# 32x32 diagonal blocks solved on GpSimd and log decays by a masked scan in a gated DeltaNet + S5 layer, on one core

## The chip, the cores and the metric

One Trainium2 chip, of which the kernel uses one core. The metric is device microseconds of one execution, the median over several. Engines: TensorE (PE) multiplies matrices, VectorE (DVE), ScalarE (ACT) and GpSimd (POOL) do elementwise work, SyncE (SP) issues nearly all DMAs. Each engine runs its own queue strictly in the order in which the program was written; semaphores hold an instruction until what it needs is there.

## The reference

One hybrid layer on x of 1024 x 2048 floats: RMSNorm, one wide input projection, an S5 branch (diagonal state space, GELU, GLU) and a gated DeltaNet branch of 8 heads, both projected up, merged by gates, projected out, added to x and normalised. The part that the change touches is the chunked delta rule:

```python
gc = jnp.cumsum(g, axis=-1)
decay = jnp.exp(jnp.where(causal, gc[..., :, None] - gc[..., None, :], -jnp.inf))
kk = jnp.einsum("bhncd,bhnsd->bhncs", k, k)
a_mat = jnp.where(strict, beta[..., None] * kk * decay, 0.0)
rhs = jnp.concatenate([v * beta[..., None], k * (beta * jnp.exp(gc))[..., None]], axis=-1)
sol = lax.linalg.triangular_solve(a_mat, rhs, left_side=True, lower=True, unit_diagonal=True)
```

g is one log decay for each frame and head. `decay` is needed as a matrix for each chunk, and the unit lower triangular matrix 1 + a_mat has to be inverted or solved with. The kernel works in chunks of 128 frames (an exact regrouping of the reference's 64).

## The kernel before

The sequence goes in two passes of 512 frames (NPASS, T), that is four chunks of 128 frames. Within a pass the program walks over blocks of 128 output columns: first the small logits, then for each of the 8 heads the columns of k, q, v, z and two blocks of gates, with one block of the S5 input between; then further gates, the up-projections and the output projection. A block is 48 matmuls of 128x128 by 128x512 for K = 2048: weights are split in a high part (whi, cut by ScalarE) and a low part (wlo, the rest, by VectorE) in fp32r, so that each pair of tiles takes three matmuls. Weights come in halves of 512 KB (raw, three buffers, w_load). A half is two chunks; a chunk is one whi and one wlo of 128x512 and feeds 12 matmuls. w_prep makes chunks four ahead of their use, into five buffers.

All the rest is laid between these matmuls by generators in lanes ("prep", "chain", "s5" and others). pump() runs after every three matmuls and lets each lane take at most one step, up to its next yield. When a step may be taken is decided by Clock and Timed: a model that is kept while the program is written, with a time for each engine (fixed cost plus a cost an element from COST; for GpSimd 0.14 us and 2.1 ns an element for a tensor_tensor) and for each cell of each tile. After a step, its lane waits until the model's TensorE has passed the model's end of what the step issued, and 0.2 us more. The model's times thus set the order of the queues; the chip then runs that order with its own times.

The head's work is in two generators. d_prep(h) (lane "prep") makes ready what the recurrence needs; d_chain(h) (lane "chain") starts when it is done and walks the four chunks through the state. d_prep runs once for each head and pass, 16 times, in these stages:

- **Decay.** GpSimd makes dhl, the causal mask times the gate (once for the high and once for the low part, gth and gtl, two chunks at a time). TensorE multiplies it with after_r (four matmuls of 128x256), ScalarE takes the exponential into E, GpSimd masks E.
- **Products.** TensorE multiplies k with k and q; VectorE multiplies with E into LU and qk, and LU with cc_ (the product "M<-M,smalls" in the rows below).
- **Block solve.** LU (128 x 4 x 128) goes to DRAM (lu_d), and its 32 diagonal blocks of 16x16 come back, one in each of 32 partitions. GpSimd inverts all of them by forward substitution in 15 steps of two instructions. The inverses and their transposes go to DRAM (tu_d, two tensors) and come back as Tm and U, block diagonal.
- **Doubling.** From 16 to 32, 32 to 64 and 64 to 128: small matmuls with LU, Tm and U, and ScalarE copies of the results. The first of them (16 to 32) takes 16 matmuls of 32x32, two VectorE products (with off16 and id32), 32 more matmuls and eight ScalarE copies.

E, LU and mi are tiles of one head at a time; kq, v, qk, U and kd exist twice, for even and odd heads. All these are pieces of one block, which the profile's rows call M. A matmul in plain fp32 is two instructions in the profile. The helpers tt, ts and stt and the wrapper Timed record nearly every operation at one line, L135, so rows are told apart by tiles and shapes.

Of the kernel before, what the change touches and what calls it, by code (L numbers as in the profile page):

```python
# [36 lines left out]
P = 128  # L37
# [110 lines left out]
def kernel(  # L148
# [49 lines left out]
    def bank(i):  # L198
        return psum.tile([P, 512], F32, tag=f"p{i}", name=nm(f"p{i}"))
# [13 lines left out]
    def tt(o, a, b, op, eng=None):  # L213
        (eng or V).tensor_tensor(o, a, b, op=op)
# [24 lines left out]
    off16 = cpool.tile([P, 2, 16], F32, name="off16")  # L239
    id32 = cpool.tile([P, 32], F32, name="id32")  # L240
    G.memset(off16, 0.0)
    for b in range(4):
        s32 = slice(32 * b, 32 * b + 32)
        G.tensor_copy(id32[s32, :], ident[s32, s32])
        G.memset(off16[s32, 0, :], -1.0)
        G.affine_select(off16[s32, 0, :], off16[s32, 0, :], pattern=[[0, 16]], compare_op=ALU.is_ge,
                        fill=0.0, base=-16, channel_multiplier=1)
    after_r = cpool.tile([P, P], F32R, name="after_r")
    S.activation(after_r, after, AF.Copy)
# [27 lines left out]
    lu_d = [dram.tile([4, 129, P], F32, name=f"lu_d{i}") for i in range(2)]  # L277
    tu_d = [[dram.tile([4, 129, P], F32, name=f"tu_d{i}{j}") for j in range(2)] for i in range(2)]
# [738 lines left out]
    gth = cpool.tile([P, 8, 4], F32, name="gth")  # L1017
    gtl = cpool.tile([P, 8, 4], F32, name="gtl")
# [4 lines left out]
    def gates_prep(lg, ps_):  # L1023
# [50 lines left out]
    dhl = cpool.tile([P, 2, P], F32R, name="dhl")  # L1074
# [16 lines left out]
    def d_prep(h, ps_):  # L1091
# [54 lines left out]
        SP.dma_start(rows(lud), LU)  # L1146
        yield
        mif = mi.rearrange("p c n -> p (c n)")
        Ef = E.rearrange("p c n -> p (c n)")
        ba = mif[0:32, 0:256].rearrange("p (i m) -> p i m", i=16)  # L1150
        btm = mif[0:32, 256:512].rearrange("p (i m) -> p i m", i=16)
        bx = Ef[0:32, 0:256].rearrange("p (i m) -> p i m", i=16)
        bu = Ef[0:32, 256:512].rearrange("p (i m) -> p i m", i=16)
# [32 lines left out]
        g3 = mi[:, :, 0:32]  # L1186
        B4 = [slice(32 * b, 32 * b + 32) for b in range(4)]
# [504 lines left out]
```

## Time and profile before

| what | value |
|---|---|
| median of three runs | 2998.08 us (2997.61 to 3001.38) |
| the profiled execution | 3000.75 us, its span 2998.7 us |
| granted TensorE clock | 0.996 |
| DMA | 405.29 MB, 135 GB/s over the span |

The profiled execution's span is from its first to its last instruction; 2.05 us lie around it. Durations below come from that execution. In a row of the timeline stand the start (us), the time that the row covers, engine, line, operation, the tiles written and read, the shape, how many instructions the row merges, and in brackets how long the engine was idle before it and what ended that. In a row of a group stand, after the count, busy us and mean ns of one instruction, then idle time before such instructions and what ended it. TensorE's instructions are pipelined: what one costs is read from the distance of starts, not from its own duration.

### The profile page before, as it was taken

What the parts mean: (1) busy time and instruction counts of PE and PEld (TensorE: products, weight loads), DVE (VectorE), ACT (ScalarE), POOL (GpSimd) and SP (SyncE); (2) the same over time, 40 slices, a digit from 0 to 9 for tenths busy, and PEclk for the clock granted to TensorE, in tenths of its full rate; (3) what the DMA queues carried; (4) which work ended last, traced back from release to release, by engine and by line L of the source; (5) the groups of instructions that cost most, each with busy time, mean ns of one, the idle gap of its engine ahead of it and who ended that gap; (6) DMA issues with size and microseconds to landing.
All of it is one profiled execution on the core that took longest, in us unless ns stands there. A gap on an engine that the chain in (4) does not pass through costs nothing.

```text
span 2998.7 us, 42470 instructions
## 1 busy us (share of the span) xinstructions
PE 2952.0 (98%) x15902; PEld 2372.9 (79%) x15902; DVE 1676.4 (56%) x3130; ACT 1149.5 (38%) x2483; POOL 460.2 (15%) x857
## 2 busy tenths in 40 slices
PE   8999999999999999999999999999999999999998
PEld 6877777777777888888878777777777788888887
DVE  5746777777767422553454676567556633226542
ACT  5434544554544222334333344333433322223331
POOL 4413222122200000000024221222122000000000
PEclk9999999999999999999999999999999999999999
DMA  6435445444545644446354444544444464445541
GB/s 166 125 79 145 115 131 135 112 123 122 135 136 161 195 119 119 145 137 239 120 162 133 116 116 117 137 120 115 123 127 122 137 198 123 118 125 155 195 149 57
DMA packets 618240, 405.29 MB, mean 135 GB/s; under 512 B 91257, under 2 KB 551218, under 8 KB 616114
## 3 DMA queue, kind: packets, MB, share of 16 engines
q1 hardware_dynamic: 615730, 394.19, 46.2%
q0 software_dynamic: 2304, 8.39, 0.8%
q8 instruction: 125, 2.05, 0.3%
q14 instruction: 81, 0.66, 0.1%
HBM read 335.79 MB, written 66.72 MB: 134 GB/s over the span
## 4 chain that ended last, share of the span: by engine, by line
PE 85%; DVE 6%; ACT 3%; POOL 2%; DMA 2%; issue 2%; SPq 1%; DVEq 0%; POOLq 0%; ACTq 0%
PE p L135 85%; DVE G0a L135 2%; DVE M L135 2%; POOL M L135 2%; DVE wlo L135 1%; ACT M L135 1%; DVE tmp L135 1%; SPq L135 1%; POOL smalls L135 1%; DMA M<-tu_d 0%; ACT tmp L135 0%; ACT whi L135 0%; ACT L135 0%; ACT G0b L135 0%; DMA raw<-in_w_in_dram 0%
## 5 line engine op out<-in xcount | busy, mean ns | idle before, releaser
L135 PE MATMUL p<-X,whi 128*128 128x512 f32 (+1 forms) x4432 | 1396.4, 397 | 1.5 <-DVE whi L135 0.8
L135 DVE TENSOR_TENSOR wlo<-raw,whi 128x512 fp32r<-128x512 f32 x920 | 633.2, 700 | 744.2 <-ACT whi L135 743.5
L135 PEld LDWEIGHTS p<-X,whi 128*128 128x128 f32 (+1 forms) x4432 | 802.0, 188 | 175.3 <-issue 17.9
L135 PE MATMUL p<-X,wlo 128*128 128x512 f32 (+1 forms) x2184 | 852.7, 390 | 0.3 <-DVE wlo L135 0.2
L135 ACT ACTIVATE whi<-raw 128x512 fp32r<-128x512 f32 x917 | 557.8, 625 | 519.0 <-PE p L135 487.2
L135 PE MATMUL p<-Y,whi 128*128 128x512 f32 (+1 forms) x1808 | 568.0, 396 | 0.9 <-ACT p L135 0.9
L135 PEld LDWEIGHTS p<-X,wlo 128*128 128x128 f32 x2184 | 410.9, 188 | 89.1 <-DVE wlo L135 0.9
L135 PEld LDWEIGHTS p<-Y,whi 128*128 128x128 f32 (+1 forms) x1808 | 330.7, 187 | 71.3 <-issue 3.9
L135 PE MATMUL p<-Y,wlo 128*128 128x512 f32 x896 | 349.7, 390 | 0.0
L135 POOL TENSOR_SCALAR smalls<-smalls 128x4 f32<-128x4 f32 (+1 forms) x58 | 18.2, 313 | 1584.8 <-DVE smalls L135 1116.3
L135 ACT ACTIVATE tmp<-p 128x512 f32<-128x512 f32 x160 | 95.5, 597 | 400.9 <-PE p L135 393.6
L135 POOL TENSOR_TENSOR M<-M 32x28 f32<-32x28 f32 (+8 forms) x492 | 196.7, 400 | 282.8 <-DMA M<-lu_d 200.1
L135 DVE TENSOR_TENSOR G0a<-G0a 128x256 f32<-128x256 f32 (+1 forms) x432 | 211.1, 525 | 7.2 <-ACT G0a L135 3.5
L135 PEld LDWEIGHTS p<-M 32*32 32x32 f32 (+2 forms) x3072 | 153.0, 123 | 72.6 <-ACT M L135 28.8
L135 PEld LDWEIGHTS p<-Y,wlo 128*128 128x128 f32 x896 | 168.1, 188 | 36.5 <-DVE wlo L135 0.4
L135 PE MATMUL p<-M 32*32 32x32 f32 (+3 forms) x3072 | 186.9, 215 | 6.9 <-DMA M<-tu_d 3.8
L135 ACT ACTIVATE M<-p 32x128 f32<-32x128 f32 (+3 forms) x337 | 98.9, 297 | 161.1 <-PE p L135 157.5
L135 DVE SCALAR_TENSOR_TENSOR tmp<-tmp,vec 128x512 f32<-128x512 f32 x144 | 112.0, 778 | 11.7 <-ACT tmp L135 8.3
L135 DVE TENSOR_TENSOR G0a<-p,G0a 128x512 f32<-128x512 f32 x128 | 82.0, 681 | 13.9 <-PE p L135 13.8
L135 DVE TENSOR_TENSOR_SCAN G0a<-rho,scar,G0a 128x256 f32<-128x256 f32 x128 | 89.3, 738 | 0.0
L135 PE MATMUL p<-whi,G0a 128*128 128x512 f32 x280 | 88.5, 391 | 0.0
L135 PE MATMUL p<-whi,X 128*128 128x512 f32 x256 | 82.2, 393 | 0.0
(209 smaller groups left out, 2640.7 us busy)
## 6 DMA issues: line engine op xcount, KB each, us to landing
raw<-in_w_in_dram SPq DMA_DIRECT2D x324, 512.0 KB, 4.0
raw<-in_w_out_dram SPq DMA_DIRECT2D x56, 512.0 KB, 4.0
raw<-in_dn_w_up_dram SPq DMA_DIRECT2D x32, 512.0 KB, 4.1
raw<-in_s_w_up_dram SPq DMA_DIRECT2D x32, 512.0 KB, 3.9
td_d<-tmp SPq DMA_DIRECT2D x32, 256.0 KB, 2.0
M<-tu_d SPq DMA_DIRECT2D x32, 256.0 KB, 3.2
cs_d<-G0a SPq DMA_DIRECT2D x32, 256.0 KB, 2.2
yg_d<-G0a SPq DMA_DIRECT2D x64, 128.0 KB, 2.4
```

What stands on the lines that cost most here:

```text
L135: return f(*a, **k)
```

## The change

Four things change, all in or around d_prep.

- **Decay by a scan.** gates_prep transposes the gates of all heads and chunks (128x32) on TensorE and writes them as rows to a small DRAM tensor, g_d. For each head one DMA reads the head's 512 gates into E, replicated over 128 partitions. VectorE then runs a tensor_tensor_scan over each chunk: state = (state + g) * strict, with strict the mask of later frames. dhl, its products on GpSimd and the four matmuls with after_r go, as do gth and gtl.
- **Blocks of 32.** The diagonal blocks are 32x32, 16 of them. Four DMAs write them to lu_d. One DMA reads each whole block (4 KB) into 8 partitions, 128 partitions in all, into E and mi together (Emi). Each partition holds four columns of the inverse, which start as columns of the identity, read from idg_d. GpSimd runs the forward substitution in 31 steps of two instructions.
- **The way back.** One DMA writes the result to tu_d, now one tensor, and one reads it as U. VectorE transposes U in blocks of 32x32 into Tm.
- **The stage from 16 to 32 goes**, with off16 and id32.

COST, LATE and WAIT, from which the order follows, stay as they were.

```diff
@@ gates_prep
-        S.activation(gth.bitcast(F32R), gt, AF.Copy)
-        tt(gtl, gt, gth, SUB, eng=G)
         p3 = bank(5)
-        for i, m in enumerate((causal, after_r.bitcast(F32), ones)):
+        PE.transpose(p3[0:32, 96:96 + P], gf, ident)
+        for i, m in enumerate((causal, afterk, ones)):
             PE.matmul(p3[:, i * 32:(i + 1) * 32], lhsT=m, rhs=gf, start=True, stop=True)
+        grow = mif[0:32, 256:256 + P]
+        S.activation(grow, p3[0:32, 96:96 + P], AF.Copy)
+        SP.dma_start(g_d[0], grow)
@@ d_prep
-        pD = bank(5)
-        for j in range(2):
-            for i, gg in enumerate((gth, gtl)):
-                tt(dhl, gg[:, h, 2 * j:2 * j + 2].unsqueeze(2).broadcast_to([P, 2, P]),
-                   causal[:, None, :].broadcast_to([P, 2, P]), MUL, eng=G)
-                yield
-                PE.matmul(pD[:, j * 256:(j + 1) * 256], lhsT=after_r, rhs=dhl.rearrange("p c n -> p (c n)"),
-                          start=(i == 0), stop=(i == 1))
-        S.activation(E.rearrange("p c n -> p (c n)"), pD, AF.Exp)
+        Ef = E.rearrange("p c n -> p (c n)")
+        SP.dma_start(Ef, part(g_d, h * 512, (0, P), (1, 512)))
+        yield
+        for c in range(4):
+            V.tensor_tensor_scan(E[:, c, :], E[:, c, :], strict, 0.0, op0=ADD, op1=MUL)
+        S.activation(Ef, Ef, AF.Exp)
         tt(E, E, hb4(causal), MUL, eng=G)
...
-        SP.dma_start(rows(lud), LU)
-        yield
...
-        SP.dma_start(ba, diag_blocks(lud))
-        G.memset(mif[0:32, 256:512], 0.0)
-        G.memset(mif[0:32, 256:512:17], 1.0)
-        yield
-        for j in range(15):
-            n = 15 - j
-            a = ba[:, j, j + 1:16].unsqueeze(2).broadcast_to([32, n, j + 1])
-            b = btm[:, j:j + 1, 0:j + 1].broadcast_to([32, n, j + 1])
-            tt(bx[:, 0:n, 0:j + 1], a, b, MUL, eng=G)
-            tt(btm[:, j + 1:16, 0:j + 1], btm[:, j + 1:16, 0:j + 1], bx[:, 0:n, 0:j + 1], SUB, eng=G)
+        for b in range(4):
+            SP.dma_start(part(lud, b * 1024, (32, 32), (4096, 4), (1, 32)),
+                         LU[32 * b:32 * b + 32, :, 32 * b:32 * b + 32])
+        yield
+        lb = dw["Emi"].rearrange("p (j t) -> p j t", j=32)
+        Uf = U.rearrange("p c n -> p (c n)")
+        iu, ix = (Uf[:, i * P:(i + 1) * P].rearrange("p (m t) -> p m t", m=4) for i in range(2))
+        SP.dma_start(dw["Emi"], part(lud, 0, (1024, 16), (0, 8), (1, 1024)))
+        SP.dma_start(Uf[:, 0:P], part(idg_d, 0, (0, 16), (P, 8), (1, P)))
+        yield
+        for j in range(31):
+            n = 31 - j
+            a = lb[:, j:j + 1, j + 1:32].broadcast_to([P, 4, n])
+            b = iu[:, :, j:j + 1].broadcast_to([P, 4, n])
+            tt(ix[:, :, 0:n], a, b, MUL, eng=G)
+            tt(iu[:, :, j + 1:32], iu[:, :, j + 1:32], ix[:, :, 0:n], SUB, eng=G)
             if j % 3 == 2:
                 yield
-        G.tensor_copy(bu, btm.rearrange("p i m -> p m i"))
-        yield
-        SP.dma_start(diag_blocks(tud[0]), btm)
-        SP.dma_start(diag_blocks(tud[1]), bu)
+        SP.dma_start(part(tud, 0, (4128, 16), (512, 8), (P, 4), (1, 32)), iu)
         stored = clock.last
...
-        SP.dma_start(Tm, rows(tud[0]))
-        SP.dma_start(U, rows(tud[1]))
-        yield
-        pG = bank(5)
+        SP.dma_start(U, rows(tud))
+        yield
+        V.transpose(Tm.rearrange("p c n -> p (c n)"), U.rearrange("p c n -> p (c n)"))
         gs = mi
-        for b in B4:
-            for c in range(4):
-                PE.matmul(pG[b, c * 32:(c + 1) * 32], lhsT=LU[b, c, b], rhs=Tm[b, c, b], start=True, stop=True)
-        tt(g3, pG[:, 0:P].rearrange("p (c n) -> p c n", c=4),
-           off16.rearrange("p a c -> p (a c)")[:, None, :].broadcast_to([P, 4, 32]), MUL)
-        tt(g3, g3, id32[:, None, :].broadcast_to([P, 4, 32]), ADD)
-        yield
-        pU = bank(2)
-        for b in B4:
-            for c in range(4):
-                PE.matmul(pU[b, c * 32:(c + 1) * 32], lhsT=g3[b, c, :], rhs=U[b, c, b], start=True, stop=True)
-                PE.matmul(pU[b, P + c * 32:P + (c + 1) * 32], lhsT=U[b, c, b], rhs=g3[b, c, :],
-                          start=True, stop=True)
-        for b in B4:
-            S.activation(U[b, :, b], pU[b, 0:P].rearrange("p (c n) -> p c n", c=4), AF.Copy)
-        for b in B4:
-            S.activation(Tm[b, :, b], pU[b, P:2 * P].rearrange("p (c n) -> p c n", c=4), AF.Copy)
         yield
```

**Where it moves instructions.** Three places in the last head of the second pass. First VectorE's queue before, from the LU product (first row) to the products on the first doubling matmuls; "M" is d_prep's block, "smalls" holds the factors cc_, "off" and "id" are off16 and id32:

```order
L135 TENSOR_TENSOR M_1692_13095<-M_1692_13095,smalls 128x512
...
L135 TENSOR_TENSOR wlo_19523<-raw_19398,whi_19522 128x512
...
L135 TENSOR_TENSOR wlo_19746<-raw_19626,whi_19745 128x512
L135 TENSOR_TENSOR wlo_19764<-raw_19626,whi_19763 128x512
L135 TENSOR_TENSOR M_1692_13095<-p_2508_19770,off_86 128x4x32
L135 TENSOR_TENSOR M_1692_13095<-M_1692_13095,id_87 128x4x32
```

And the same stretch of VectorE's queue after the change, from the LU product to the transpose that makes Tm:

```order
L135 TENSOR_TENSOR M_1668_12823<-M_1668_12823,smalls 128x512
...
L135 TENSOR_TENSOR wlo_18999<-raw_18814,whi_18998 128x512
...
L135 TENSOR_TENSOR wlo_19342<-raw_19241,whi_19341 128x512
L135 TENSOR_TENSOR M_1668_12823<-p_2469_19348,smalls 128x512
L135 TENSOR_TENSOR wlo_19366<-raw_19241,whi_19365 128x512
L135 STREAM_TRANSPOSE M_1668_12823<-M_1668_12823 128x512
```

Between the two ends stand 10 wlo rows before and 15 now (first and last are shown; an S5 head's work stands among them in both). The products with off and id are gone.

Second, SyncE's queue in the same head before, from the write of LU to the reads of the inverses; "raw" are weight halves:

```order
L135 DMA lu_d_125<-M_1692_13095 128x4x128
L135 DMA G0a_12942<-cs_d 128x512
L135 DMA M_1692_13095<-lu_d_125 32x16x16
L135 DMA raw_19570<-in_w_in_dram 128x8x128
...
L135 DMA raw_19690<-in_w_in_dram 128x8x128
L135 DMA tu_d_128<-M_1692_13095 32x16x16
L135 DMA tu_d_129<-M_1692_13095 32x16x16
L135 DMA yg_d<-G0a_12942 64x2x256 x4
L135 DMA M_1692_13095<-tu_d_128 128x4x128
L135 DMA M_1692_13095<-tu_d_129 128x4x128
```

And after:

```order
L135 DMA lu_d_112<-M_1668_12823 32x4x32 x4
L135 DMA raw_19023<-in_w_in_dram 128x8x128
L135 DMA M_1668_12823<-lu_d_112 128x1x1024
L135 DMA M_1668_12823<-idg_d 128x1x128
...
L135 DMA raw_19071<-in_w_in_dram 128x8x128
...
L135 DMA raw_19290<-in_w_in_dram 128x8x128
L135 DMA tu_d_114<-M_1668_12823 16x32x32
L135 DMA raw_19339<-in_w_in_dram 128x8x128
L135 DMA M_1668_12823<-tu_d_114 128x4x128
```

Three weight halves stood between the read of LU and the reads of the inverses, six stand there now, one of them between the write and the read.

Third, TensorE's queue before, where the result of the solve is first used ("p" is PSUM, 32x32 rows are the small matmuls, the others belong to the projection):

```order
L135 MATMUL p_2508_19770<-M_1692_13095 32x32 x16
L135 MATMUL p_2505_19762<-Y_1453_11621,whi_19692 128x512 x2
...
L135 MATMUL p_2509_19799<-M_1692_13095 32x32 x32
L135 MATMUL p_2505_19762<-Y_1453_11621,whi_19715 128x512 x2
...
L135 MATMUL p_2513_19855<-M_1692_13095 32x32 x8
```

And after:

```order
L135 MATMUL p_2470_19364<-Y_1429_11349,wlo_19315 128x512
L135 MATMUL p_2476_19396<-M_1668_12823 32x32 x8
L135 MATMUL p_2470_19364<-Y_1429_11349,whi_19314 128x512 x2
...
L135 MATMUL p_2477_19413<-M_1668_12823 32x32 x16
```

The groups of 16 and 32 small matmuls are gone; the group of 8, from 32 to 64, is now the first that uses the result.

More of the change, by code (lines that the diff above doesn't have):

```diff
@@ L238 @@
                     channel_multiplier=1)
[L239 to L249, printed above, removed]
+    afterk = cpool.tile([P, P], F32, name="afterk")
+    S.activation(afterk, after, AF.Copy)
+    strict = cpool.tile([P, P], F32, name="strict")
+    tt(strict, causal, ident, SUB, eng=G)
     halfpi = cpool.tile([P, 1], F32, name="halfpi")
@@ L275 @@
     cs_d = dram.tile([32, P, 512], F32, name="cs_d")
-    lu_d = [dram.tile([4, 129, P], F32, name=f"lu_d{i}") for i in range(2)]
-    tu_d = [[dram.tile([4, 129, P], F32, name=f"tu_d{i}{j}") for j in range(2)] for i in range(2)]
+    lu_d = [dram.tile([4, 4, 1024], F32, name=f"lu_d{i}") for i in range(2)]
+    tu_d = [dram.tile([4, 129, P], F32, name=f"tu_d{i}") for i in range(2)]
+    idg_d = dram.tile([1, 32, 32], F32, name="idg_d")
+    g_d = dram.tile([1, 32, P], F32, name="g_d")
     nq_d = [dram.tile([1, P, 16], F32, name=f"nq_d{i}") for i in range(2)]
@@ L287, in part @@
         return bass.AP(tensor=a.tensor, offset=a.offset + off, ap=[list(x) for x in dims])
-    def diag_blocks(d):
-        a = d[:, :, :]
-        return bass.AP(tensor=a.tensor, offset=a.offset, ap=[[16 * P + 16, 32], [P, 16], [1, 16]])
     def rows(d):
@@ L1009, in d_views @@
             dw["set"].append(s)
-        dw["E"] = tk(512).rearrange("p (c n) -> p c n", c=4)
         dw["LU"] = tk(512).rearrange("p (c n) -> p c n", c=4)
-        dw["mi"] = tk(512).rearrange("p (c n) -> p c n", c=4)
+        dw["Emi"] = tk(1024)
+        dw["E"] = dw["Emi"][:, 0:512].rearrange("p (c n) -> p c n", c=4)
+        dw["mi"] = dw["Emi"][:, 512:1024].rearrange("p (c n) -> p c n", c=4)
         dw["ch"] = tk(512)
     gt = cpool.tile([P, 8, 4], F32, name="gt")
-    gth = cpool.tile([P, 8, 4], F32, name="gth")
-    gtl = cpool.tile([P, 8, 4], F32, name="gtl")
     bt = cpool.tile([P, 8, 4], F32, name="bt")
@@ L1072, in gates_prep @@
         yield -1
-    dhl = cpool.tile([P, 2, P], F32R, name="dhl")
     nk = [small(f"nk{i}", 4) for i in range(2)]
@@ L1145, in d_prep @@
         yield
-        SP.dma_start(rows(lud), LU)
+        for b in range(4):
+            SP.dma_start(part(lud, b * 1024, (32, 32), (4096, 4), (1, 32)),
+                         LU[32 * b:32 * b + 32, :, 32 * b:32 * b + 32])
         yield
[L1148 to L1153, printed above, removed]
-        SP.dma_start(ba, diag_blocks(lud))
-        G.memset(mif[0:32, 256:512], 0.0)
-        G.memset(mif[0:32, 256:512:17], 1.0)
-        yield
-        for j in range(15):
-            n = 15 - j
-            a = ba[:, j, j + 1:16].unsqueeze(2).broadcast_to([32, n, j + 1])
-            b = btm[:, j:j + 1, 0:j + 1].broadcast_to([32, n, j + 1])
-            tt(bx[:, 0:n, 0:j + 1], a, b, MUL, eng=G)
-            tt(btm[:, j + 1:16, 0:j + 1], btm[:, j + 1:16, 0:j + 1], bx[:, 0:n, 0:j + 1], SUB, eng=G)
+        lb = dw["Emi"].rearrange("p (j t) -> p j t", j=32)
[3 more added lines that the diff above has]
+        SP.dma_start(Uf[:, 0:P], part(idg_d, 0, (0, 16), (P, 8), (1, P)))
+        yield
+        for j in range(31):
[4 more added lines that the diff above has]
+            tt(iu[:, :, j + 1:32], iu[:, :, j + 1:32], ix[:, :, 0:n], SUB, eng=G)
             if j % 3 == 2:
                 yield
-        G.tensor_copy(bu, btm.rearrange("p i m -> p m i"))
-        yield
-        SP.dma_start(diag_blocks(tud[0]), btm)
-        SP.dma_start(diag_blocks(tud[1]), bu)
+        SP.dma_start(part(tud, 0, (4128, 16), (512, 8), (P, 4), (1, 32)), iu)
         stored = clock.last
@@ L1179, in d_prep @@
         yield stored
-        SP.dma_start(Tm, rows(tud[0]))
-        SP.dma_start(U, rows(tud[1]))
+        SP.dma_start(U, rows(tud))
         yield
-        pG = bank(5)
+        V.transpose(Tm.rearrange("p c n -> p (c n)"), U.rearrange("p c n -> p (c n)"))
         gs = mi
-        g3 = mi[:, :, 0:32]
-        B4 = [slice(32 * b, 32 * b + 32) for b in range(4)]
-        for b in B4:
-            for c in range(4):
-                PE.matmul(pG[b, c * 32:(c + 1) * 32], lhsT=LU[b, c, b], rhs=Tm[b, c, b], start=True, stop=True)
-        tt(g3, pG[:, 0:P].rearrange("p (c n) -> p c n", c=4),
-           off16.rearrange("p a c -> p (a c)")[:, None, :].broadcast_to([P, 4, 32]), MUL)
-        tt(g3, g3, id32[:, None, :].broadcast_to([P, 4, 32]), ADD)
-        yield
-        pU = bank(2)
-        for b in B4:
-            for c in range(4):
-                PE.matmul(pU[b, c * 32:(c + 1) * 32], lhsT=g3[b, c, :], rhs=U[b, c, b], start=True, stop=True)
-                PE.matmul(pU[b, P + c * 32:P + (c + 1) * 32], lhsT=U[b, c, b], rhs=g3[b, c, :],
-                          start=True, stop=True)
-        for b in B4:
-            S.activation(U[b, :, b], pU[b, 0:P].rearrange("p (c n) -> p c n", c=4), AF.Copy)
-        for b in B4:
-            S.activation(Tm[b, :, b], pU[b, P:2 * P].rearrange("p (c n) -> p c n", c=4), AF.Copy)
         yield
@@ L1323, in zero_tu @@
     def zero_tu():
-        for a in tu_d:
-            for b in a:
-                SP.dma_start(rows(b), ztile.rearrange("p (c n) -> p c n", c=4))
+        for b in tu_d:
+            SP.dma_start(rows(b), ztile.rearrange("p (c n) -> p c n", c=4))
+        SP.dma_start(idg_d[0], ident[0:32, 0:32])
     def out_gen(yr, oss, r0):
```

## The prediction

> **What bounds the kernel now.** I read the page first, then who waits for whom, then TensorE's own timeline.
>
> ```profile
> span 2998.7 us, 42470 instructions
> PE 2952.0 (98%) x15902; PEld 2372.9 (79%) x15902; DVE 1676.4 (56%) x3130; ACT 1149.5 (38%) x2483; POOL 460.2 (15%) x857
> PE   8999999999999999999999999999999999999998
> PE 85%; DVE 6%; ACT 3%; POOL 2%; DMA 2%; issue 2%; SPq 1%; DVEq 0%; POOLq 0%; ACTq 0%
> ```
>
> TensorE (PE) is busy in every slice and carries 85% of the chain that ended last. VectorE (DVE) and GpSimd (POOL) have room. So two things count: how long PE stands on work that goes, and where PE will newly wait.
>
> ```profile
> PE p L135 <- DMA M<-tu_d: 3.8, 5, 0.8
> PEld p L135 <- POOL dhl L135: 6.2, 15, 0.8
> PEld p L135 <- ACT whi L135: 8.5, 22, 0.9
> ```
>
> These are the only PE waits near the change: us in total, times, the longest. PE almost never waits for the solve's result (tu_d), so the order around it fits the machine, but by how much it fits has to be found.
>
> **What PE gets back.** PE's rows in one head of the first pass:
>
> ```profile
> 423.74 0.39 PE L135 MATMUL p<-X,wlo 128*128 128x512 f32 x1
> 424.06 0.89 PE L135 MATMUL p<-M 32*32 32x32 f32 x32
> 424.88 0.73 PE L135 MATMUL p<-X,whi 128*128 128x512 f32 x2
> ...
> 427.41 0.40 PE L135 MATMUL p<-X,wlo 128*128 128x512 f32 x1
> 427.74 1.91 PE L135 MATMUL p<-M 32*32 32x32 f32 x64
> 429.57 0.73 PE L135 MATMUL p<-X,whi 128*128 128x512 f32 x2
> ...
> 430.37 0.63 PE L135 MATMUL p<-X,whi 128*128 128x512 f32 x2
> 430.84 0.39 PE L135 MATMUL p<-X,wlo 128*128 128x512 f32 x1
> 431.06 0.62 PE L135 MATMUL p<-X,whi 128*128 128x512 f32 x2
> ```
>
> Three projection matmuls start 0.69 us apart (430.37 to 431.06), so one costs 0.23. The group of 32 instructions (16 matmuls, two instructions each) costs 424.88 - 423.74 - 0.23 = 0.91 us of PE's time, the group of 64 costs 429.57 - 427.41 - 0.23 = 1.93. Both go, in 16 heads: 16 x 2.84 = **45.4 us**.
>
> The decay matrix loses four 128x256 matmuls a head, 64 in all. Each is half as wide as a projection matmul, 0.11 us: 7.2, and with the 6.2 us of waits for dhl **13.4 us**. The 3.8 us of waits for tu_d go too, but the same transfer is waited for in another place, below. Sum: 62.6 us. The transpose of the gates that gates_prep gains is one small matmul a pass, nothing here.
>
> **What the new solve takes on POOL.** It replaces 30 instructions of 15 to 64 elements by 62 of 4 x n elements, n from 31 to 1 (2 x 4 x 496 = 3968 elements). No row shows a form of that kind; the nearest:
>
> ```profile
> 1593.37 0.61 POOL L135 TENSOR_TENSOR dhl<-gth,causal 128x256 fp32r<-128x256 f32 x1 [0.90 <-PE p L135]
> 1599.05 1.02 POOL L135 TENSOR_TENSOR smalls<-smalls,minus 128x4 f32<-128x4 f32 x1
> 1600.15 0.20 POOL L135 TENSOR_TENSOR smalls<-smalls,bt 128x4 f32<-128x4 f32 x1
> 1620.07 11.53 POOL L135 TENSOR_TENSOR M<-M 32x15 f32<-32x15 f32 x30 [17.57 <-DMA M<-lu_d]
> 1886.09 14.79 POOL L135 TENSOR_TENSOR M<-M 32x15 f32<-32x15 f32 x30 [15.91 <-DMA M<-lu_d]
> 2287.39 14.52 POOL L135 TENSOR_TENSOR M<-M 32x15 f32<-32x15 f32 x30 [17.76 <-DMA M<-lu_d]
> ```
>
> A product of 4 elements takes 0.20 us, one of 256 takes 0.61: 1.63 ns an element on 0.19, and 0.08 between two (1599.05 + 1.02 to 1600.15). By that the old 30 (1360 elements) take 30 x 0.27 + 2.2 = 10.3 us, the new 62 take 62 x 0.27 + 6.5 = 23.3. The old ones really take 11.5 to 14.8, and DVE's load says why:
>
> ```profile
> 312.00:344.00 32.00, 32.00 (x273) 24.98 (x272) 25.71 (x55) 16.78 (x35) 13.34 (x32) 1.00 0.45 129
> 1620.00:1631.60 11.60, 11.60 (x55) 9.18 (x54) 2.71 (x5) 2.73 (x5) 9.25 (x30) 1.00 0.91 275
> 1886.00:1901.00 15.00, 15.00 (x73) 11.83 (x72) 7.82 (x15) 5.60 (x10) 12.57 (x31) 1.00 0.49 141
> 2288.00:2318.00 30.00, 29.16 (x230) 23.12 (x229) 12.08 (x22) 10.32 (x24) 12.67 (x30) 1.00 0.57 157
> ```
>
> The columns are the stretch, its length, then busy time of PE, PEld, DVE, ACT and POOL. With DVE busy 2.71 us the 30 lose 1.2 us against 10.3, with 7.82 they lose 4.5: about 0.5 us for each us of DVE. The 30 us that the new solve would fill in a late head have 12.08 us of DVE, so 23.3 + 5.5 = **28.8 us** in the second pass. In the first pass DVE is twice as busy (25.71 in 32), but POOL already shares with it at the worst rate seen, 14.8 / 10.3 = 1.43; I take 1.36, **31.8 us**. Bounds: 23.3 if nothing collides, 33.4 if everything does at 1.43.
>
> The Trainium skill, "GPSIMD Engine Reference", section 3.1 (Elementwise — side-by-side cycle accounting), puts a two-input GpSimd operation at about 2.6 cycles an element, 2.2 ns at the page's 1.2 GHz. Against the 1.63 ns of these rows its estimate for the solve would be some 2 us longer; the rows decide.
>
> **How long the order lets it take.** VectorE makes one wlo for every 12 projection matmuls, 12 x 0.23 = 2.7 us of PE, so its queue is a clock. In the last head 10 wlo rows stand between the LU product (M<-M,smalls) and the first use of the solve's result (M<-p,off): 27 us. After the change 15 rows stand between the LU product and the new transpose. Counted over the heads: before 9 to 11 (one head 14), after 13, 24, 15, 15, 16, 17, 16, 16 in the first pass and 16, 15, 16, 15, 15, 15, 15, 15 in the second. 15 rows are 40.8 us, and the first matmul on the result stands 0.7 us further on: 41.5.
>
> ```profile
> 2281.14 0.40 SPq L135 DMA_DIRECT2D lu_d<-M  x1
> 2285.39 0.32 SPq L135 DMA_DIRECT2D M<-lu_d  x1
> 2306.00 1.14 SPq L135 DMA_DIRECT2D M<-tu_d  x2
> 2309.26 0.87 PE L135 MATMUL p<-M 32*32 32x32 f32 x32 [0.84 <-DMA M<-tu_d]
> raw<-in_w_in_dram SPq DMA_DIRECT2D x324, 512.0 KB, 4.0
> M<-tu_d SPq DMA_DIRECT2D x32, 256.0 KB, 3.2
> tu_d<-M SPq DMA_DIRECT2D x32, 32.0 KB, 1.7
> L135 DVE STREAM_TRANSPOSE M<-M 128x512 f32<-128x512 f32 x16 | 11.2, 701 | 0.0
> L135 DVE TENSOR_TENSOR_SCAN G0a<-rho,scar,G0a 128x256 f32<-128x256 f32 x128 | 89.3, 738 | 0.0
> ```
>
> Today: 2281.14 to 2309.26 is 28.1 us, and PE waits the last 0.84. The clock of rows is right within 1 us. After the change the same way is: four small LU writes, 0.4 apart, the last landing 1.7 later (2.9); the 512 KB replicated read (4.0 like a weight load); POOL; the write (1.7) and one 256 KB read (3.2); the transpose (0.7); some 0.9 between steps. That is 13.4 us beside POOL: 42.2 in the second pass, 45.2 in the first. Against 41.5 PE is 0.7 late in each of six second-pass heads, 4 us. In the first pass: the first head (13 rows, 36.1 us; before the S5 work fills DVE, so at 42.2) 6 late, two heads with 15 rows 3.7 each, three with 16 rows (44.2) 1.0 each, the two with 17 and 24 none: 16. As a row count is cut off by half a row (1.3 us) on average, part of that is not there. I take **12 us** of new waits, ends 0 (POOL 23.3) and 66 (POOL 33.4: 37 in the second pass, 29 in the first).
>
> The Clock itself gives the solve only 62 x 0.14 us + 3968 x 2.1 ns = 17 us. The order leaves more, because three of its steps are handed out at a time, between groups of PE work, and each batch waits for the Clock's PE to pass the one before. While PE waits for the solve, its own queue stands still. Behind the transposing DVE stand the wlo of chunks that PE needs four chunks (11 us) later, so a lateness under that costs PE once. Behind the solve's write SyncE has one weight load and the read of the result; that load is needed three halves later, 16 us, against 4 to land.
>
> **The rest, costed at nothing.** DVE gains four scans (half of 738 ns each) and a transpose, loses two small products: 1.6 us a head on an engine at 56%. ACT loses eight copies; PE waited 8.5 us for ACT in all, so the gain is between 0 and that. The decay load (256 KB, about 3.2 us) is issued as soon as the head before has freed E, and hidden by that lead; if it were not, the chain of the head before would stand behind the scans on DVE, at most 16 x 3.2 = 51 us. POOL loses the dhl products.
>
> **Sum.** The profiled run took 3000.75 us, 2.05 around its span. 3000.75 - 62.6 + 12 = 2950; that run is 2.67 over the median of the three, so **2947 us**.
>
> **Rivals.** *The solve is late everywhere and PE hands back the gain* (slower). For: POOL stretched by 1.43 beside a busy DVE, and longer operations meet more DVE instructions. Against: behind today's solve DVE is lightly loaded (12.08 in 30 us). The point is a solve of about 33 us, 0.53 us an instruction with its gap: then the waits reach 60 us, 2996. At 36 us it is 3 more in 15 heads, 3041. The Trainium skill, "SBUF — State Buffer" (SBUF: two separate sides), says that a DVE operation with two SBUF inputs and a GpSimd operation hold a shared port pair by turns, each for a whole instruction. The stretched runs agree; how far it reaches with the new form no run here shows.
>
> *Late in part*: solves of 30.5 to 33 us, or the decay load showing: 27 to 58 us of waits, 2962 to 2993.
>
> *No change*: what goes on PE is filled by another bound, such as weights through ACT and DVE. Against it stands a PE that waits 8.5 us for ACT in 2998. 2998.
>
> **Chances.** Forecast (2935 to 2960) 0.60, late in part 0.18, no change 0.08, slower 0.14. A measurement of this kernel tells some 0.2% (6 us) from no change. Faster 0.78, same 0.08, slower 0.14. The range runs from 2932 (no waits, and some of ACT's gain) to 2996.
>
> **What would show it.** The costliest-groups view of TensorE:
>
> ```profile
> L135 PE MATMUL p<-M 32*32 32x32 f32 x2304 | 64.1, 193 | 4.1 <-DMA M<-tu_d 3.8 <-ACT M L135 0.2
> ```
>
> This group falls from 2304 to 768 instructions (24 of 72 matmuls a head stay), with none on dhl. The solve's 62 instructions take 27 to 32 us a head. PE's (or DVE's) wait for M<-tu_d stays near a us a head. I am wrong if that wait is over 4 us a head, if single new POOL instructions pass 0.5 us, or if wlo waits grow.

## The result, and the profile after

| | median of its runs, us | against before, 95% interval |
|---|---|---|
| before | 2999.02 (2997.61 to 3001.38) | |
| changed | 3018.4 (3013.54 to 3023.04) | 1.0064 (1.0041 to 1.0086) |

The changed kernel is 19 us slower; 2947 was forecast, and the range ended at 2996. The profiled execution took 3022.74 us. Its page: span, busy time of each engine, and the shares of the chain that ended last.

```profile
span 3019.6 us, 39590 instructions
PE 2941.1 (97%) x14304; PEld 2361.7 (78%) x14304; DVE 1706.5 (57%) x3178; ACT 1104.5 (37%) x2349; POOL 625.1 (21%) x1243
PE 62%; POOL 14%; DVE 9%; DMA 7%; issue 5%; ACT 2%; SPq 1%; DVEq 0%; POOLq 0%; ACTq 0%
```

1598 TensorE instructions are gone, but its busy time fell by only 10.9 us (2952.0 to 2941.1), and the chain runs 14% over GpSimd, where it was 2%. TensorE's groups with shapes kept apart (behind the second bar the idle time ahead of them), then TensorE's waits (us, times, longest):

```profile
L135 PE MATMUL p<-M 32*32 32x32 f32 x768 | 23.0, 216 | 33.3 <-DVE M L135 33.3
```

```profile
PE p L135 <- DVE M L135: 46.7, 24, 5.2
```

The 32x32 group has the 768 instructions that were expected, and 33.3 us of idle time ahead of it, where it was 4.1. It waits for the transpose on VectorE, which waits for the solve's result. The timeline of the last head of the second pass shows how (SyncE's queue, GpSimd, VectorE and TensorE; start, length, idle time before in brackets):

```profile
2295.71 1.75 SPq L135 DMA_DIRECT2D lu_d<-M  x4
...
2298.74 0.55 SPq L135 DMA_DIRECT2D M<-lu_d  x1
2299.35 0.59 SPq L135 DMA_DIRECT2D M<-idg_d  x1
...
2305.70 30.56 POOL L135 TENSOR_TENSOR M<-M 128x124 f32<-128x124 f32 x62 [16.32 <-DMA M<-idg_d]
...
2336.28 0.57 SPq L135 DMA_DIRECT2D tu_d<-M  x1
...
2339.10 0.39 PE L135 MATMUL p<-Y,wlo 128*128 128x512 f32 x1
...
2342.02 0.71 DVE L135 STREAM_TRANSPOSE M<-M 128x512 f32<-128x512 f32 x1 [6.69 <-DMA M<-tu_d]
2342.79 0.59 PE L135 MATMUL p<-M 32*32 32x32 f32 x16 [3.30 <-DVE M L135]
2343.31 0.99 PE L135 MATMUL p<-Y,whi 128*128 128x512 f32 x2
...
2348.20 1.05 PE L135 MATMUL p<-X,whi 128*128 128x512 f32 x2
...
2351.38 0.63 PE L135 MATMUL p<-X,whi 128*128 128x512 f32 x2
```

From the first LU write to the first 32x32 matmul 47.1 us pass, 3.30 of them TensorE's wait. Then the same two projection matmuls take 1.05 us at 2348.20 and 0.63 at 2351.38. The windows view says why; its third number from the end is TensorE's granted clock:

```profile
2343.00:2350.00 7.00, 7.00 (x64) 4.84 (x61) 1.25 (x4) 2.25 (x7) 0.00 (x0) 0.54 0.56 181
2351.00:2355.00 4.00, 4.00 (x24) 3.04 (x23) 0.69 (x1) 1.02 (x3) 0.00 (x0) 1.00 0.42 118
```

**TensorE works at half clock for 7 us behind the wait**, and is "busy" all that time: the waits view doesn't show it. After the first 60 us the changed kernel has 12 such stretches of 3.4 to 13.7 us, 119.5 us in all; before has two, 6.8 us. Eleven of the twelve follow a wait of 1.4 to 4.8 us ahead of the 32x32 matmuls; the only other wait there, of 0.98 us, is followed by none. The mean granted clock falls from 0.996 to 0.978 (of 3019.6 us, 66 us of full clock missing against 12).

So three numbers are needed of each trace: TensorE's idle time (all its gaps up to its last instruction), the loss at half clock (half of the time that the clock's records after the first 60 us show at 0.5, without the part of gaps that falls into it), and the rest of the span, its work at full clock (with some 9 us after its last instruction). In us:

| kernel | span | idle | of it ahead of 32x32 | half-clock stretches | loss by them | work |
|---|---|---|---|---|---|---|
| before | 2998.7 | 38.0 | 4.1 | 2 | 3.4 | 2957.3 |
| changed | 3019.6 | 69.9 | 33.3 | 12 | 58.3 | 2891.3 |
| difference | +20.8 | +31.9 | +29.2 | +10 | +54.9 | -66.0 |

Half is an upper bound: by the distance of starts between neighbours of the same shapes, inside and outside of the stretches, the changed kernel loses 51 us there and before 3, and the work falls by 59 us in place of 66.

The gain came. It was handed back once in waits, and once more, and dearer, in clock.

### The profile page after: what moved, and what is told of

Same layout as the page of the kernel before. It is cut to its first block, busy times and chain, and to the rows that moved or that the text cites. A ratio compares the mean times of both kernels' runs of the same rounds, so it can differ in the third digit from the quotient of the medians.

```text
span 3019.6 us, 39590 instructions
## 1 busy us (share of the span) xinstructions
PE 2941.1 (97%) x14304; PEld 2361.7 (78%) x14304; DVE 1706.5 (57%) x3178; ACT 1104.5 (37%) x2349; POOL 625.1 (21%) x1243
## 4 chain that ended last, share of the span: by engine, by line
PE 62%; POOL 14%; DVE 9%; DMA 7%; issue 5%; ACT 2%; SPq 1%; DVEq 0%; POOLq 0%; ACTq 0%
PE p L135 62%; POOL M L135 13%; DVE M L135 3%; DVE G0a L135 2%; DMA M<-idg_d 2%; DVE wlo L135 2%; DMA M<-tu_d 1%; SPq L135 1%; ACT M L135 1%; DMA raw<-in_w_in_dram 1%; DMA tu_d<-M 1%; DVE tmp L135 1%; DMA smalls<-nq_d 1%; POOL ex L135 1%; DMA lu_d<-M 1%
## 5 line engine op out<-in xcount | busy, mean ns | idle before, releaser
L135 DVE TENSOR_TENSOR wlo<-raw,whi 128x512 fp32r<-128x512 f32 x920 | 640.7, 710 | 712.2 <-ACT whi L135 710.6
L135 PEld LDWEIGHTS p<-X,whi 128*128 128x128 f32 (+1 forms) x4432 | 818.1, 190 | 176.9 <-issue 14.0
L135 PE MATMUL p<-X,wlo 128*128 128x512 f32 (+1 forms) x2184 | 861.6, 395 | 0.2 <-DVE wlo L135 0.2
L135 PE MATMUL p<-Y,whi 128*128 128x512 f32 (+1 forms) x1808 | 576.4, 401 | 0.9 <-ACT p L135 0.9
L135 POOL TENSOR_TENSOR M<-M 128x32 f32<-128x32 f32 (+30 forms) x1004 | 431.1, 429 | 285.4 <-DMA M<-idg_d 161.6
L135 PEld LDWEIGHTS p<-M 32*32 32x32 f32 (+2 forms) x1536 | 120.7, 155 | 108.4 <-DVE M L135 52.7
L135 PE MATMUL p<-M 32*32 32x32 f32 (+3 forms) x1536 | 150.8, 256 | 44.7 <-DVE M L135 38.3
L135 ACT ACTIVATE M<-p 32x128 f32<-32x128 f32 (+3 forms) x195 | 55.7, 291 | 189.9 <-PE p L135 170.2
L135 POOL TENSOR_TENSOR M<-M,causal 128x512 f32<-128x512 f32 x16 | 22.4, 1401 | 389.3 <-ACT M L135 389.3
```

The source lines that it names most:

```text
L135: return f(*a, **k)
```

## The experiments

**Theory:** the placing model gives the solve 17 us and its replicated read a weight load's time, so the first matmuls on the result are placed 1 to 5 us early; TensorE waits, and behind the waits its clock is halved. **Rivals:** the waits alone; the load that the change puts on VectorE, GpSimd and SyncE; the decay scan. All kernels, ordered as told (idle time, stretches and work are those of the profiled execution, which can lie some us off the median):

| kernel | median, us | against before, 95% interval | idle (ahead of 32x32) | stretches, their loss | work |
|---|---|---|---|---|---|
| scan_only | 2993.8 | 0.9982 (0.9972 to 0.9991) | 38.7 (4.3) | 2, 4.5 | 2945.3 |
| blocks_only | 2991.2 | 0.9972 (0.9953 to 0.9991) | 63.7 (28.1) | 9, 27.3 | 2902.9 |
| true_dur | 3138.0 | 1.0464 (1.0449 to 1.0480) | 190.1 (0.1) | 9, 52.2 | 2898.6 |
| td_late | 2945.8 | 0.9823 (0.9806 to 0.9839) | 43.1 (0.0) | 4, 8.1 | 2892.8 |
| td3_13 | 2939.7 | 0.9802 (0.9787 to 0.9816) | 39.6 (4.6) | 2, 7.8 | 2893.2 |
| dose_30_0 | 2958.1 | 0.9864 (0.9848 to 0.9881) | 52.1 (9.5) | 3, 5.3 | 2897.2 |
| fill10 | 2990.4 | 0.9973 (0.9964 to 0.9983) | 47.4 (9.2) | 5, 16.8 | 2931.9 |
| fill_behind | 3027.4 | 1.0091 (1.0076 to 1.0106) | 74.9 (35.7) | 8, 17.9 | 2932.9 |
| idg_early | 3006.8 | 1.0017 (0.9997 to 1.0038) | 69.3 (30.6) | 12, 53.9 | 2890.4 |
| late_before | 3094.5 | 1.0323 (1.0298 to 1.0347) | 88.7 (58.0) | 14, 48.7 | 2950.2 |

### Each part alone

scan_only takes only this into the kernel before (and what feeds it), blocks_only puts the old lines back into the changed one:

```diff
-        pD = bank(5)
-        for j in range(2):
-            for i, gg in enumerate((gth, gtl)):
...
-                PE.matmul(pD[:, j * 256:(j + 1) * 256], lhsT=after_r, rhs=dhl.rearrange("p c n -> p (c n)"),
...
+        SP.dma_start(Es, part(g_d, h * 512, (0, P), (1, 512)))
+        yield
+        for c in range(4):
+            V.tensor_tensor_scan(E[:, c, :], E[:, c, :], strict, 0.0, op0=ADD, op1=MUL)
```

> The kernel before with the decay part of the change alone (scan of the replicated log decays, no dhl matmuls); the solve of 16x16 blocks stays. Theory (the loss comes from the solve's result arriving late, each TensorE wait of over about 1 us being followed by 3 to 14 us at half clock): 13 us faster than before, 2980 to 2992, with no more half-clock stretches than before's two after the start. Rival (the scan and its replicated read on SyncE cause the loss): 3000 or more, with new TensorE waits.

> The changed kernel with the old decay matrix (dhl matmuls back); 32x32 blocks on GpSimd stay. Theory: the changed kernel's time plus the 13 us of the dhl work, 3022 to 3042, with ten or more half-clock stretches after waits on the solve's result. Rival (the scan causes the loss): 2950 to 2990.

scan_only is 5 us faster, not 13 (its profiled execution, the fastest of ten, is 10 us faster than before's): TensorE's work fell by 12.0 us, but the new order holds one wait for wlo of 10.6 us. SyncE stood on a table's write, with a weight load behind it:

```profile
214.81 0.37 SPq L135 DMA_DIRECT2D w_d<-G0b  x1
229.40 0.37 SPq L135 DMA_DIRECT2D ft_d<-Y  x1
229.87 4.40 SPq L135 DMA_DIRECT2D raw<-in_w_in_dram  x2
```

blocks_only was missed: 2991, not 3022 to 3042, and close to the rival's 2950 to 2990. Its waits ahead of the 32x32 matmuls come to nearly the changed kernel's (28.1 against 33.3 us), but they fall on seven heads with over 1 us instead of eleven, and the loss at half clock is 27 us instead of 58. In work the parts add up (-12.0 and -54.4; both together, in the changed kernel, -66.0). In time they don't: 5 and 8 us faster alone, 19 slower together. The scan alone isn't the culprit. That the loss of both together hangs on the placing is not shown by these two; td3_13, below, shows it.

### Fill the wait, or the time behind it

fill10, in d_prep; fill_behind has the same loop behind the eight matmuls, into bank 6:

```diff
         pG = bank(5)
+        for i in range(10):
+            nc.tensor.matmul(pG[:, (i % 4) * P:(i % 4 + 1) * P], lhsT=ident, rhs=causal, start=True, stop=True)
         pg = pG.rearrange("p (c n) -> p c n", c=4)
```

> The changed kernel with ten 128x128 matmuls of constants on TensorE ahead of the first 32x32 matmuls of each head, into the same bank, which are overwritten; the order is else the same. About 2 us a head, in which TensorE works where it stood waiting. Theory (half clock follows waits): waits on the solve fall from 33 to about 10 us, the ten matmuls cost 16 x 2.1 = 34 us, so 11 us more of both; but most half-clock stretches vanish, 51 falls to 10 to 20 us of loss: 2980 to 3005 in all. Rival (the clock falls by itself in this stretch, by the small matmuls or the change's load, not by waits): 3025 to 3040.

> The changed kernel with fill10's ten matmuls of constants behind the first eight 32x32 matmuls of each head instead of ahead of them, into a bank of their own: the waits stay, the same 39 us of work is added. Theory (half clock comes from TensorE's stand with the little use behind it): waits stay near 30 us and most stretches at half clock stay, some shorter: 3030 to 3060. Rival (fill10 was faster because ten dense matmuls raise TensorE's use near the small ones, not because they stood in the wait): 2985 to 3010 again.

The last head of fill10, then of fill_behind, on TensorE:

```profile
2319.04 2.39 PE L1174 MATMUL p<-causal,ident 128*128 128x128 f32 x20
2322.29 0.59 PE L135 MATMUL p<-M 32*32 32x32 f32 x16 [0.86 <-DVE M L135]
2322.81 0.74 PE L135 MATMUL p<-Y,whi 128*128 128x512 f32 x2
2323.39 0.40 PE L135 MATMUL p<-Y,wlo 128*128 128x512 f32 x1
2323.63 0.63 PE L135 MATMUL p<-Y,whi 128*128 128x512 f32 x2
```

```profile
2348.07 0.59 PE L135 MATMUL p<-M 32*32 32x32 f32 x16 [2.98 <-DVE M L135]
2348.59 4.13 PE L1180 MATMUL p<-causal,ident 128*128 128x128 f32 x20
2352.47 0.71 PE L135 MATMUL p<-Y,whi 128*128 128x512 f32 x2
```

fill10 gives TensorE some 40 us more to do (16 heads, 2.39 us in the row above) and is 28 us faster than the changed kernel: a wait of 0.86 instead of some 3 us, and the pair behind it takes 0.63. Its idle time is only 22.5 us less, so the waits alone would have made it slower: the halved clock is a cost of its own.

fill_behind keeps the waits (35.7 us) and is 9 us slower than the changed kernel, a little under the 3030 to 3060 expected. So in time the rival falls that dense matmuls anywhere near help as much. For the clock the rival stands: the loss is 17.9 us, nearly fill10's 16.8, where the changed kernel has 58.3. The wait of 2.98 us in the last head is still followed by half clock, but for 3.4 us where the changed kernel has 6.8, and just over the ten matmuls, which take 4.13 us there and 2.39 in fill10. In the windows view:

```profile
2348.80:2352.20 3.40, 3.40 (x17) 3.40 (x17) 0.00 (x0) 0.49 (x2) 0.00 (x0) 0.50 0.87 287
```

What follows a wait takes part in how long the clock stays down.

### Late without the change

```diff
+        for i in range(4):
+            nc.gpsimd.tensor_tensor(scr, ones[:, 0:4], pexp["minus"], op=ALU.pow)
         G.tensor_copy(bu, btm.rearrange("p i m -> p m i"))
```

> The kernel before, where the solve ends 4 us later: four small powers on GpSimd (about 1 us each) ahead of the last copy of each head's solve, unknown to the placing model, so the order is the same. Nothing else of the change. Theory: with the 0 to 0.8 us by which six heads already wait, TensorE waits 2 to 4.5 us in most of 16 heads, 35 to 60 us in all, and 8 or more new half-clock stretches cost 30 to 60 more: 3060 to 3110. Rival (waits alone, the half clock came from the change's load on VectorE, GpSimd and DMA): 3030 to 3050, with before's two stretches. Rival (there is room for 4 us): within 5 us of before.

```profile
PE p L135 <- DMA M<-tu_d: 58.0, 16, 5.2
```

In the kernel before, 4 us of small powers on GpSimd make all 16 heads wait, and the span grows by 88.9: 50.7 of idle time and 45.3 at half clock, less 7.1 in the rest. The work is the same, so the half overstates the loss by about that. No part of the change's load is there, and the clock falls in 14 places all the same.

### The identity read earlier

```diff
         SP.dma_start(nq_d[h % 2][0], qs_[:, 0:16])
+        SP.dma_start(U.rearrange("p c n -> p (c n)")[:, 0:P], part(idg_d, 0, (0, 16), (P, 8), (1, P)))
...
-        SP.dma_start(Uf[:, 0:P], part(idg_d, 0, (0, 16), (P, 8), (1, P)))
```

> The changed kernel, with the identity's read (M<-idg_d) issued ahead of the reads of nq_d instead of behind the replicated read; the placing stays nearly the same. Theory: GpSimd starts 1 to 2 us sooner a head, as it waited for this read in 12 of 16; waits on the solve fall from 33 to 10 to 20 us, and some of the 12 half-clock stretches vanish with the waits that fall under 1 us: 2965 to 3000. Rival (waits alone): 13 to 23 us off, 2995 to 3005; rival (the replicated read is as late): no change.

GpSimd's group in the changed kernel, then in idg_early (behind the second bar its idle time and what ended it):

```profile
L135 POOL TENSOR_TENSOR M<-M 128x32 f32<-128x32 f32 (+30 forms) x1004 | 431.1, 429 | 285.4 <-DMA M<-idg_d 161.6 <-DVE wlo L135 40.7 <-DMA raw<-in_w_in_dram 3.6
```

```profile
L135 POOL TENSOR_TENSOR M<-M 128x32 f32<-128x32 f32 (+30 forms) x1004 | 429.3, 428 | 280.3 <-DMA M<-lu_d 121.9 <-DVE G0a L135 24.9 <-DVE wlo L135 21.4
```

A miss: only the name of the last transfer changed. The replicated read lands nearly as late as the identity, waits fell by 2.7 us and not by 13 to 23, and the stretches stayed at 12. Its median is 12 us under the changed kernel's, but its ten runs lie between 2984 and 3015 us, and the profiled one is the slowest; the four of td3_13 below lie within 5.

### Tell the placing model the durations

true_dur (td3_13 has 3.0 and 0.13, dose_30_0 has 3.0 and 0); td_late is true_dur with the last line:

```diff
         SP.dma_start(Uf[:, 0:P], part(idg_d, 0, (0, 16), (P, 8), (1, P)))
+        for cl in clock.cells(dw["Emi"]):
+            clock.wr[cl] += 4.0
+        clock.last += 4.0
         yield
...
             tt(ix[:, :, 0:n], a, b, MUL, eng=G)
+            clk["G"] += 0.2
             tt(iu[:, :, j + 1:32], iu[:, :, j + 1:32], ix[:, :, 0:n], SUB, eng=G)
+            clk["G"] += 0.2
+            for cl in clock.cells(iu):
+                clock.wr[cl] += 0.2
+            clock.last += 0.2
...
-LATE = (1.0, 1.4)
+LATE = (1.6, 2.0)
```

> The changed kernel, with the placing model told what the solve's way takes: each of the 62 instructions 0.2 us longer (17 becomes 29.4 us) and the replicated read 4 us later. The same instructions, in another order: by the order some 51 us of TensorE work stand between the read's issue and the first 32x32 matmul, where the changed kernel has 39 to 46. Theory: waits on the solve fall from 33 to under 6 us, half-clock stretches from 107 to under 20 us, time 2935 to 2955. Rival 1 (the waits alone are the price, the rest of the loss is load on VectorE, GpSimd and SyncE): 33 us off, 2980 to 2990. Rival 2 (the heads, placed later, are late at the chain instead): 2990 or more, with waits on state or M in the chain.

true_dur took 3138 us, where 2935 to 2955 was expected. Its waits ahead of the 32x32 matmuls are gone, as forecast (0.1 us), yet this stands in its windows, and in TensorE's waits:

```profile
1216.00:1390.00 174.00, 49.05 (x139) 21.68 (x136) 120.41 (x273) 35.84 (x68) 4.53 (x8) 0.50 0.21 66
```

```profile
PE p L135 <- DVE G0a L135: 77.8, 19, 7.1
```

For 174 us TensorE is busy 49, at half clock, and waits for VectorE's S5 work. The heads, placed later, counted as late; the rule in step then refuses the S5 lane, and its rest was run in one piece behind the projections. Two runs test that, and a third a part of the durations:

> As true_dur with its full durations, and one line more: the rule that calls a head late allows 0.6 of a block more (LATE 1.6 and 2.0 for 1.0 and 1.4). Theory for true_dur's 3138 us: the rule refused the S5 stage while heads were late, and 135 of its steps were run in one piece at the end of the first pass, at half clock; with the rule loosened that goes, and the time is 2935 to 2965. Rival (the later placing of the solve costs the time by itself): 3050 or more.

> As true_dur, with less: each of the 62 instructions 0.13 us longer in the placing model (25 us in all), the replicated read 3 us later. By the order 43 to 52 us of TensorE work stand ahead of each head's first 32x32 matmuls, and no stage is left over to be run in one piece at the end of the pass. Theory (in the changed kernel waits cost 33 us and half clock behind them some 50): TensorE's work at full clock stays 2896 us, all its gaps come to 36 to 46, the loss at half clock to under 10: 2935 to 2950. Rival (heads that are placed later run late elsewhere, or the load on GpSimd and VectorE is the price): 2965 or more.

> As td3_13, with only the replicated read told (3 us later), not the solve's instructions. By the order about 3 us more of TensorE work stand ahead of the 32x32 matmuls than in the changed kernel, 3 to 7 less than in td3_13. Theory: the waits of 1 to 4 us fall to under 1 us in most heads, 33 us in all to 3 to 12, and the half clock's 50 us to 0 to 20: 2940 to 2970. Rival (what td3_13 gained hangs on the solve's instructions being told): above 2985.

All three came out as the theory has it. One line on lateness takes 192 us off true_dur. td3_13, with milder durations and the old rule, runs the changed kernel's instructions in 2939.7 us, 2% under before; TensorE's waits, and the timeline of the last head:

```profile
PE p L135 <- DVE M L135: 14.8, 9, 5.2
```

```profile
2223.74 0.55 SPq L135 DMA_DIRECT2D M<-lu_d  x1
...
2228.78 31.65 POOL L135 TENSOR_TENSOR M<-M 128x124 f32<-128x124 f32 x62 [2.38 <-DVE M L135]
...
2275.11 0.71 DVE L135 STREAM_TRANSPOSE M<-M 128x512 f32<-128x512 f32 x1 [4.01 <-DMA M<-tu_d]
...
2277.26 0.59 PE L135 MATMUL p<-M 32*32 32x32 f32 x16
2277.78 0.73 PE L135 MATMUL p<-Y,whi 128*128 128x512 f32 x2
```

From the read's issue to the first matmul it has 53.5 us, of which the transpose leaves 1.4; the changed kernel had 44.1 with 3.3 of waiting in it. The solve is no shorter (31.65 us) and VectorE, GpSimd and SyncE have the same work, so the rival of load falls. The work is 2893.2 us, within 2 of the changed kernel's. The read's 3 us alone (dose_30_0) bring 60 of the 79 us between the changed kernel and td3_13.

### What halves the clock

Neither micro kernel computes the layer, and each ran once; both run dense 128x512 matmuls with one disturbance every 25 to 35 us.

> Not the computation: dense runs of 128x512 matmuls (110 to 131, some 25 to 30 us) with one TensorE wait between them on a ScalarE copy of 128 to 4608 elements (waits of about 0.6 to 5 us), seven lengths four times each; then two lengths followed by groups of 16 small 32x32 matmuls among dense ones, and 48 small ones without a wait. The outputs are left out. Theory: waits under 1 us leave the clock at full, those over 1.5 us halve it mostly, for 3 to 14 us whatever their length; small matmuls without a wait leave it. Rival 1: only waits of 3.4 us or more halve it. Rival 2: the small matmuls halve it.

> Not the computation (outputs left out): dense runs of 128x512 matmuls; between them, four times each, a wait of about 1.2 or 1.5 us on ScalarE, with and without what follows a wait in the kernel (16 small 32x32 matmuls, 6 dense, 32 small, 6 dense); the same group without a wait; 96 small ones without a wait. Theory, after micro (1.1 and 1.5 us alone: 0 of 8 halved; with small groups behind: 5 of 8, for 10 to 14 us): wait and group together halve the clock in 4 or more of 8, for 7 us or more; wait alone in none of 8; group alone in none of 4. Rival (the small groups alone do it): group alone and the 96 in most of 8.

How often a stretch at half clock followed, and how long it was:

| disturbance | halved | us at half clock |
|---|---|---|
| wait 0.8, 1.1, 1.5 us (micro), 1.2, 1.5 us (micro2), dense behind | 0 of 20 | |
| wait 1.9 us, dense behind | 1 of 4 | 3.4 |
| wait 2.4 us | 2 of 4 | 3.4 |
| wait 3.2 us | 3 of 4 | 3.4 |
| wait 4.5 us | 4 of 4 | 3.4, once 6.8 |
| wait 1.1 us, then 3 x 16 small matmuls, 4 dense between | 2 of 4 | 10.2, 13.7 |
| wait 1.5 us, the same behind | 3 of 4 | 10.2, 13.7, 13.7 |
| wait 1.2 or 1.5 us, then 16 small, 6 dense, 32 small, 6 dense | 4 of 8 | 3.4, once 10.2 |
| the same group without a wait | 0 of 4 | |
| 48 small in a row (3.2 us), no wait | 0 of 4 | |
| 96 small in a row (7 us), no wait | 4 of 4 | 6.8, once 10.2 |

Two of them. First, in micro, a wait of 1.50 us with small groups behind, in the timeline and then in windows (the stretch, its length, busy time of PE, PEld, ACT and POOL, then the clock):

```profile
290.84 0.50 PE L209 MATMUL pm<-hi,gate 128*128 128x512 f32 x1 [1.50 <-ACT gate L208]
291.28 1.23 PE L202 MATMUL ps<-raw 32*32 32x32 f32 x32
...
294.45 1.91 PE L202 MATMUL ps<-raw 32*32 32x32 f32 x32
```

```profile
290.90:292.20 1.30, 1.30 (x30) 1.05 (x31) 0.00 (x0) 0.00 (x0) 1.00 0.00 0
292.30:305.90 13.60, 13.60 (x92) 10.46 (x89) 0.00 (x0) 0.00 (x0) 0.50 0.01 1
306.00:316.00 10.00, 10.00 (x46) 8.26 (x45) 0.00 (x0) 0.00 (x0) 1.00 0.01 2
```

Then the 96 small ones of micro2 (two instructions each), in the same two views:

```profile
223.62 7.33 PE L202 MATMUL ps<-raw 32*32 32x32 f32 x192
```

```profile
228.00:234.80 6.80, 6.80 (x69) 5.95 (x66) 0.00 (x0) 0.00 (x0) 0.51 0.00 0
```

I had the threshold too simple. With dense work behind it a wait of 1.9 to 4.5 us can halve the clock, and mostly costs one stretch of 3.4. The traces also tell which waits do: in each trace all half-clock records start on one grid with steps of 3.413 us. Of the 36 waits with dense work behind, the ten that halved the clock stood 1.9 us or more inside one step of that grid. The other 26, one of them 3.2 us long, stood at most 1.7 us in any one step.

Standing and small 32x32 matmuls work together: with small groups behind, 1.1 us is enough in 2 of 4 cases of micro. The stretch is 10 to 14 us there, but 3.4 in three of four cases of micro2, where 7 or more was expected. Enough small ones do it alone, so the rival was half right. The kernel puts its waits exactly ahead of such groups (32x32, then 64x64). That fits its waits of 1.4 to 4.8 us, which are followed by up to 13.7 us at half clock; what sets the length of a stretch is not shown.

## Why the prediction was wrong, step by step

- **What TensorE gets back, 62.6 us** (52.6 of work, 10 of waits): right, and the work a little more than that. It fell by 66.0 us (59 by the distance of starts): 54.4 by the blocks alone (45.4 forecast), 12.0 by the decay matmuls (7.2).
- **The solve, 28.8 us in the second pass, 31.8 in the first:** 30.6 and 32.1 on average over eight heads each, near. Three heads of the first pass took 33.3 to 34.9, past the rival's point of 33. It was not needed to be slower: the second pass, with 30.0 to 32.2, holds 16.2 of the 33.3 us of waits.
- **The rest of the way, 13.4 us:** mis-sized; in the last head 47.1 - 30.56 = 16.5. The read was priced as a weight load of the same size, 4.0 us; from its issue to GpSimd's start it took 7.0 (2298.74 to 2305.70), and without the identity's read behind it (idg_early) still 6.2.
- **What the order allows, 41.5 us:** 43.8 in the last head (47.1 less the wait), so 2.3 more. Need and room together make 3.3 us late where 0.7 was forecast.
- **New waits, 12 us (0 to 66):** 33.3, inside the bounds. The error is the difference of two numbers near 45, and so it is large against the 12.
- **The rest, costed at nothing:** for the decay load that holds, as scan_only has 38.7 us of idle time against before's 38.0. But the 6.2 us of waits for dhl did not come back as time, for one wait of 10.6 us for wlo took their place.
- **The term that was missing: TensorE's clock behind a wait.** A wait was priced at its own length. The runs show it priced again: 48 to 55 us at half clock, by the way of counting, for 33.3 of waits. This is the step that failed. With it the sum closes: 2950, and 29.9 more of idle time (+31.9 measured, +2 forecast), 13.4 less of work, 54.9 at half clock, is 3021; the profiled run took 3022.7. The parts are cut from one span, so that they close proves nothing; what counts is that without the clock the sum is 2967, inside the range.
- **The rivals:** none had the mechanism. "Late in part" has the waits right (27 to 58 us) and ends at 2993, because it too leaves the clock out. "Slower" was to come from a solve of 33 us or more; it came with solves of 30.6 and 32.1.
- **The signs:** the group of 768 came as named. The wait is 2.1 us a head on average, with one over the 4 named (4.82), and six solves are over the 32 named (up to 34.9). One sign against was there: in the last head 19 of the 62 GpSimd instructions pass 0.5 us. It tells little, as 11 of the old 30 do so too. None of these names the larger part of the loss. The sign to watch, the granted clock, was not among them, though before's row of it (0.996, two stretches) could be read.

That the loss is the placing's and not the new algorithm's is shown by td3_13 and td_late; that a late solve does the same without the change, by late_before. That the small groups alone don't set it off is shown by micro2 (after a wait they halved the clock in 4 of 8 cases, without one in 0 of 4) and by td3_13, which runs the same groups with one wait of over 1 us ahead of them (4.6 us, followed by one of its two stretches). fill10 beside fill_behind doesn't show it, as both lose the same at half clock. Not settled is which head is hit in a given run.

## What to carry to other kernels

Where an order is made by a table of durations, a new operation needs its measured time in the table before it is judged: the same instructions took 3018 and 2940 us. A wait of TensorE ahead of small matmuls is to be priced at its length and up to half of a following 3 to 14 us, so read the granted clock beside the waits, and the room at each place and not its average: 1.4 us were enough in td3_13's last head. And look at what else reads the table: here truer, longer durations set off a lateness rule that cost 192 us.

## What the runs showed of the hardware

- The clock's records at 0.5 last 3.413 us or multiples of it (but for one at the end of the program), whatever the length of the wait, and their starts lie on one grid of 3.413 us in each trace; a pair of wide matmuls takes 1.05 us in them and 0.63 outside. By the Trainium skill, "TensorE: Matmul & The Clock Gate" (What's actually happening), a free-running window of 3.413 us decides, and an idle window brings half rate: the records' lengths and starts agree, but 1.9 us of standing in a window were enough in micro. The same page (HAM oscillation — how this bites in real kernels) has gaps of more than about 3.4 us as the ones to avoid. That limit does not hold here: with dense work behind it 1.9 us did it once in four, ahead of small matmuls 1.1 us twice in four.
- Busy is not use: 7 us of 32x32 matmuls without a gap halved the clock in 4 of 4 cases.
- A kernel whose waits sit near that limit varies from run to run (idg_early 2984 to 3015, blocks_only 2980 to 3005), while td3_13 stays within 2938 to 2943. The spread is the clock's: idg_early's fastest run had 0.990 granted and its slowest 0.979, which is some 33 us of full clock for 31 us of time. That the window's place against the waits does this fits micro, but no run set that place.
